# Loads of the start in another order, early products in fours, and half-length conv taps as direct sums

## The chip, the cores and the metric

The kernel runs on one core of one Trainium2 chip. The metric is the device time of one execution in microseconds (us), the median of several. Each engine of the core has its own queue of instructions, run in order: TensorE (PE: matmuls, and transposes as matmuls with an identity), VectorE (DVE), ScalarE (ACT), GpSimd (POOL), and SyncE (SP), which issues the DMAs here. A semaphore holds an instruction, and everything behind it in its queue, until what it needs is done.

## What is computed

Two layers (DEPTH 2) over 1024 tokens of width 1024, in fp32. The lines of the reference that matter (the conv has 31 taps on 512 channels, the one of the feed-forward part 3 taps on 5632):

```python
h = rms_norm(x, pre_mix_norm[l])
z = jnp.einsum("bsd,dc->bsc", h, w_in[l])
...
u = c_a * jax.nn.sigmoid(c_g)
u = causal_dwconv(u, conv_w[l], conv_b[l])
u = jax.nn.silu(layer_norm(u, conv_ln_g[l], conv_ln_b[l]))
...
o = diff_attention(q1, q2, k1, k2, v, lam)
o = rms_norm(o, subln_g[l]) * (1.0 - lam_init)
...
m = jnp.einsum("bsc,cd->bsd", jnp.concatenate([u, o], axis=-1), w_out[l])
x = x + rms_norm(m, post_mix_norm[l])
h = rms_norm(x, pre_ffn_norm[l])
up = jnp.einsum("bsd,df->bsf", h, w_up[l])
up = causal_dwconv(up, ffn_conv_w[l], ffn_conv_b[l])
g, val = jnp.split(up, 2, axis=-1)
f = jnp.einsum("bsf,fd->bsd", jax.nn.gelu(g, approximate=True) * val, w_down[l])
x = x + rms_norm(f, post_ffn_norm[l])
```

## The kernel before

Every fp32 product is three products of rounded parts (high by high, high by low, low by high). A weight is split by ACT, which writes the high part, and by POOL or DVE, which subtracts it for the low part; an activation likewise, with the low part on DVE.

**Start.** Tokens go in 8 tiles of 128 (x0 to x7). `prenorm` takes one: ACT squares it and sums (L357), DVE and POOL make the factor (L347, L349), DVE scales it in place with the gain gb (L359), PE transposes it in 8 pieces (L364), ACT copies the high part (L366) and DVE subtracts for the low part (L367), into hA (tokens 0 to 511) or hB (512 to 1023). The loads of x0 to x2 (into two buffers "y" and one "xr"), of the identity, of gb, of the causal mask nmask, of cos and sin, and of the layer's small parameters (`params`: conv weights, biases, lambda vectors) are issued first on SP, the first weights behind them.

**Mix stage.** It is written through a planner, `Flow`: generators yield the instructions of one piece each, and the planner, with a table of costs per engine, lets a filling queue, timed pieces and the queue of conv taps take turns; the order of PE, DVE, ACT and POOL is what it writes, while SP's order is left to a scheduler. The queue `TAPS = "0a 0b 1w 2w 3a 3b"` gives the conv of the four channel tiles: 0 and 3 as two halves of 512 tokens ("a", "b"), 1 and 2 whole ("w"). A tap piece is let in when DVE's clock in the plan is not ahead of PE's by more than 0.15 to 0.25 us.

`conv_taps` makes the 31-tap sum from even and odd samples (a fast filter for two phases): the sum of even and odd (`xsum`, L573), then three sums A, B and C of 16, 15 and 16 taps on half as many columns (L597), of which ACT makes the first of each (L591), and three instructions that put them together (L600, L603, L606). For a half (512 tokens) these are 48 DVE instructions on about 256 columns and 3 on ACT; for a whole part, on 512 columns. The buffers are two of a ring "y", which x0 and x1 use at the start.

After the taps `conv_fin` transposes, `conv_ln` normalises (z, L1036), and `w_out` (pw, L499) follows with attention beside it. At its end ACT and DVE make yn, the normalised input of the feed-forward stage: its last tiles by L1185.

**Feed-forward stage.** The up-projection takes 22 pairs of columns n, each with seven block products (numbered 1 to 7) in place of eight, on blocks of 512 channels by 512 tokens and their sums. Products 1 and 2 use the first 512 tokens alone (b11 and b21, the two halves of the channels); the others use sums with the second 512 tokens (b22, t1 to t4). For the 8 pairs in `EARLY`, products 1 and 2 are done ahead, as "e1" and "e2", both into the PSUM tile px. They run while yn of the later tokens is made. A product is 12 matmuls of 512 columns in the trace (L1609). `seq` put them two pairs at a time: e1 e1 e2 e2. The transposes of yn's four later tiles (`norm_t`, L1357) stand at the slots `NORM_T` of this sequence; `norm_c` then makes their parts in four steps of DVE and ACT (L1372 to L1391) for the products on t1 to t4 and b22. `e_copy` copies each px to SBUF (ACT L1462, L1464) into one of `ACC_BUFS` = 3 buffers of 1024 columns and, once both halves are there, writes it out with a DMA of 512 KB (L1465), to be fetched again later.

Of the kernel before, what the change touches and what calls it, by code (L numbers as in the profile page):

```python
# [9 lines left out]
F32 = mybir.dt.float32  # L10
F32R = mybir.dt.float32r
AF = mybir.ActivationFunctionType
# [41 lines left out]
NORM_T = (2, 5, 8, 11)  # L54
# [159 lines left out]
def build(tc, ap, out):  # L214
# [7 lines left out]
    with ExitStack() as top:  # L222
# [28 lines left out]
        first_x = lambda t: load_x(xin[t], ("y", "y", "xr")[t % 3])  # L251
# [10 lines left out]
        ve.tensor_copy(nmaskr, nmask)  # L262
        cos = const("cosT", [P, 8, 8])
        sy.dma_start(cos, ap["cos"])
        sin = const("sinT", [P, 8, 8])
        sy.dma_start(sin, ap["sin"])
# [3 lines left out]
        def params(l):  # L270
# [6 lines left out]
            cw, cv, sg = ptile("cw", [P, 4, CK]), ptile("cv", [P, 3, 4]), ptile("sg", [P, 1])  # L277
            sy.dma_start(cw, ap["cw"][l])
            sy.dma_start(cv, ap["cvec"][l])
            sy.dma_start(sg, ap["subg"][l])  # L280
            lv = par.tile([P, 4, HD], F32, tag="lv", name="lv", bufs=1)
            sy.dma_start(lv, ap["lamv"][l:l + 1].broadcast_to([P, 4, HD]))
            cws, hv, ls, nl = ptile("cws", [P, 4, (CK + 1) // 2]), ptile("hv", [P, 2, 4]), ptile("ls", [P, 2]), ptile("nl", [P, 1])
            pars[l] = dict(cw=cw, cws=cws, cv=cv, hv=hv, sg=sg, nl=nl)
# [129 lines left out]
        for l in range(DEPTH):  # L414
            xres = xin if l == 0 else x2[l - 1]
            with ExitStack() as st:
# [4 lines left out]
                if l == 0:  # L421
                    for t in range(8):
                        late[t] = prenorm(ptr, x0[t] if t < 3 else first_x(t), g_pre, hh[t // 4], t % 4)
                if l == 0:
                    for _ in params(0):
                        pass
# [130 lines left out]
                def conv_taps(ct, part):  # L557
# [9 lines left out]
                    n0, n1 = bs[0] * 256, (bs[-1] + 1) * 256  # L567
                    n = n1 - n0
                    c = dv(n, 0.123)
                    iy = yield from R["y"].get()  # L570
                    scr = xs.tile([P, YW], F32, tag="y", name="scr", bufs=2)
                    xsum, bb = scr[:, 0:n + 15], scr[:, n + 15:2 * n + 16]
                    ve.tensor_tensor(xsum, ev[:, n0:n1 + 15], od[:, n0:n1 + 15], op=ALU.add)  # L573
                    fl.op("dve", c)
                    yield 0
                    iac = iy
# [1285 lines left out]
```

## Time and profile before

| | us |
|---|---|
| median of 3 runs (2315.09 to 2317.93) | 2316.41 |
| the profiled execution | 2314.21 |
| its span | 2312.4 |

The profile is of one execution. Its page gives busy time by engine; the windows give busy time in a stretch; the list of waits says what an engine's idle time ended with; the time lines give single instructions, each with its start, its duration and in brackets the idle time ahead of it. An instruction's duration reaches past the start of the next where the engine overlaps them, so the cost of one in a row is the distance between starts.

### The profile page before, as it was taken

What the parts mean: (1) busy time and instruction counts of PE and PEld (TensorE: products, weight loads), DVE (VectorE), ACT (ScalarE), POOL (GpSimd) and SP (SyncE); (2) the same over time, 40 slices, a digit from 0 to 9 for tenths busy, and PEclk for the clock granted to TensorE, in tenths of its full rate; (3) what the DMA queues carried; (4) which work ended last, traced back from release to release, by engine and by line L of the source; (5) the groups of instructions that cost most, each with busy time, mean ns of one, the idle gap of its engine ahead of it and who ended that gap; (6) DMA issues with size and microseconds to landing.
All of it is one profiled execution on the core that took longest, in us unless ns stands there. A gap on an engine that the chain in (4) does not pass through costs nothing. (4 is left out here: it accounts for less than half of the span.)

```text
span 2312.4 us, 31516 instructions
## 1 busy us (share of the span) xinstructions
PE 2202.4 (95%) x10568; PEld 1838.5 (80%) x10568; DVE 1879.3 (81%) x3287; ACT 1126.7 (49%) x2458; POOL 832.6 (36%) x894
## 2 busy tenths in 40 slices
PE   6999997999999999999889999979999999999998
PEld 5898895878877878788778988868788778787886
DVE  6988988667888888777889889896678888887777
ACT  4445456655444444444534545465554444445443
POOL 3324312245444545201533333122454554442024
PEclk9999997999999999999999999979999999999999
DMA  4313323454333343933433123235533343348353
GB/s 156 86 48 92 79 72 123 164 206 138 119 120 130 111 137 130 316 96 111 135 100 103 41 82 97 73 114 191 194 118 124 119 136 123 104 168 274 96 164 118
DMA packets 140129, 295.39 MB, mean 128 GB/s; under 512 B 16832, under 2 KB 33984, under 8 KB 139456
## 3 DMA queue, kind: packets, MB, share of 16 engines
q1 hardware_dynamic: 139968, 293.39, 39.7%
q8 instruction: 83, 1.36, 0.3%
q14 instruction: 78, 0.64, 0.1%
HBM read 198.44 MB, written 78.12 MB: 120 GB/s over the span
## 5 line engine op out<-in xcount | busy, mean ns | idle before, releaser
L1660 PE MATMUL pd<-wp,wo 128*128 128x512 f32 x1776 | 414.2, 395 | 4.8 <-DVE wp L1305 2.8
L1660 PEld LDWEIGHTS pd<-wp,wo 128*128 128x128 f32 x1776 | 333.9, 188 | 81.7 <-DVE wp L1305 3.6
L1609 PE MATMUL py<-t,wo 128*128 128x512 f32 x1584 | 381.8, 394 | 5.8 <-DVE cg L1477 5.8
L1609 PEld LDWEIGHTS py<-t,wo 128*128 128x128 f32 x1584 | 296.8, 188 | 77.4 <-ACT wo L1304 9.0
L1305 POOL TENSOR_TENSOR wo<-ws,wo 128x512 fp32r<-128x512 f32 x176 | 249.9, 1432 | 279.5 <-ACT wo L1304 274.1
L1609 PE MATMUL px<-hA,wo 128*128 128x512 f32 x1056 | 255.3, 394 | 0.0
L1305 POOL TENSOR_TENSOR wo<-raw,wo 128x512 fp32r<-128x512 f32 x132 | 181.4, 1378 | 166.1 <-ACT wo L1304 157.3
L1609 PEld LDWEIGHTS px<-hA,wo 128*128 128x128 f32 x1056 | 198.6, 189 | 44.5 <-ACT ea L1464 0.5
L1305 POOL TENSOR_TENSOR wo<-fa,wo 128x512 fp32r<-128x512 f32 x66 | 103.1, 1577 | 323.0 <-ACT wo L1304 293.9
L1304 ACT ACTIVATE wo<-ws 128x512 fp32r<-128x512 f32 x176 | 108.8, 627 | 136.7 <-PE py L1609 47.4
L1495 DVE SCALAR_TENSOR_TENSOR acc<-cg,fw,acc 128x512 f32<-128x512 f32 x176 | 132.6, 754 | 41.7 <-ACT acc L1483 38.1
L597 DVE SCALAR_TENSOR_TENSOR scr<-u,cw,scr 128x256 f32<-128x256 f32 (+2 forms) x288 | 158.0, 565 | 3.7 <-ACT scr L591 3.6
L852 ACT ACTIVATE e<-S,mxv 128x512 f32<-128x512 f32 (+2 forms) x192 | 110.1, 581 | 64.6 <-DVE mxv L847 41.2
L1483 ACT ACTIVATE acc<-cg,fb,fw 128x512 f32<-128x512 f32 x88 | 68.2, 774 | 148.8 <-DVE cg L1477 148.8
L857 POOL TENSOR_TENSOR sm<-sm 128x1 f32<-128x1 f32 x64 | 25.5, 398 | 316.9 <-ACT e L852 301.6
L499 PE MATMUL pq<-whq,hA 128*128 128x384 f32 x512 | 135.5, 346 | 3.9 <-ACT whq L463 3.9
L499 PE MATMUL pq<-whq,hB 128*128 128x384 f32 x512 | 133.9, 342 | 0.0
L1609 PE MATMUL pz<-b,wo 128*128 128x512 f32 x528 | 129.8, 394 | 1.9 <-DVE cv L1477 1.9
L1609 PE MATMUL pz<-t,wo 128*128 128x512 f32 x528 | 128.7, 392 | 0.0
L1609 PEld LDWEIGHTS pz<-b,wo 128*128 128x128 f32 x528 | 98.4, 188 | 27.4 <-issue 5.1
L843 DVE TENSOR_REDUCE mxv<-S 128x1 f32<-128x512 f32 (+2 forms) x192 | 100.5, 549 | 24.1 <-PE S L827 18.2
L1609 PEld LDWEIGHTS pz<-t,wo 128*128 128x128 f32 x528 | 99.1, 188 | 22.7
(279 smaller groups left out, 5027.2 us busy)
## 6 DMA issues: line engine op xcount, KB each, us to landing
raw<-in_wupd SPq DMA_DIRECT2D x104, 512.0 KB, 3.6
fa<-f SPq DMA_DIRECT2D x154, 256.0 KB, 2.7
f<-fs SPq DMA_DIRECT2D x88, 256.0 KB, 3.3
raw<-in_wmix SPq DMA_DIRECT2D x80, 256.0 KB, 3.0
f<-gg SPq DMA_DIRECT2D x66, 256.0 KB, 2.0
raw<-in_wmix SPq DMA_DIRECT2D x64, 192.0 KB, 2.4
qs<-sth SPq DMA_DIRECT2D x64, 128.0 KB, 2.4
os<-onT SPq DMA_DIRECT2D x16, 512.0 KB, 3.2
```

The source lines that it names most:

```text
L499: mm = pe.matmul(dst, a, b, start=first and k + j == 0, stop=final and k == n - 1 and j == 2)
L597: ve.scalar_tensor_tensor(dst, src, wk, dst, op0=ALU.mult, op1=ALU.add)
L843: ve.tensor_reduce(mv_[:, j:j + 1], S, axis=AX.X, op=ALU.max, negate=True)
L852: se.activation(e[:, c0:c0 + w], S, AF.Exp, bias=mv_[:, 0:1], accum_out=sm[:, j:j + 1])
L857: po.tensor_tensor(sm[:, 0:1], sm[:, 0:1], sm[:, 1:2], op=ALU.add)
L1304: se.activation(w[:, 0], raw, AF.Copy)
L1305: eng.tensor_tensor(w[:, 1], raw, f32(w[:, 0]), op=ALU.subtract)
L1483: se.activation(acc[n, v, hf], C[n][v][:, 2 + hf * HB:2 + hf * HB + HB], AF.Identity, bias=fb[:, mt:mt + 1], scale=fw[:, mt, 2:3])
L1495: ve.scalar_tensor_tensor(dst, c[:, j + hf * HB:j + hf * HB + HB], fw[:, mt, j:j + 1], a, op0=ALU.mult, op1=ALU.add)
L1609: pe.matmul(ps, x, y, start=first and k + j == 0, stop=k == 3 and j == 2, skip_group_check=not first)
L1660: pe.matmul(ps[tt], x, y, start=first and k + n == 0, stop=k == K2 - 1 and n == 2, skip_group_check=not first)
```

## The change

Three parts.

1. Start: x0 to x3 are loaded at once (x3 into the second "xr" buffer). The loads of the parameters, cos, sin and nmask move behind the first four weight loads, and the cast of nmask and the arithmetic on the parameters into a timed piece of the planner.

```diff
-        first_x = lambda t: load_x(xin[t], ("y", "y", "xr")[t % 3])
+        first_x = lambda t: load_x(xin[t], ("y", "y", "xr", "xr")[t % 4])
...
-        x0 += [first_x(1), first_x(2)]
-        nmask = xs.tile([P, P], F32, tag="m0", name="nmask", bufs=4)
-        sy.dma_start(nmask, ap["nmask"])
+        x0 += [first_x(1), first_x(2), first_x(3)]
+        nmask = const("nmask", [P, P])
         nmaskr = const("nmaskr", [P, P], mybir.dt.bfloat16)
-        ve.tensor_copy(nmaskr, nmask)
...
+                def constants():
+                    yield 1.0
+                    next(par0)
+                    sy.dma_start(cos, ap["cos"])
+                    sy.dma_start(sin, ap["sin"])
+                    sy.dma_start(nmask, ap["nmask"])
+                    yield 7.0
+                    next(par0, None)
+                    ve.tensor_copy(nmaskr, nmask)
+                    fl.op("dve", 1.8)
```

2. Taps: the halves ("a", "b") are direct sums over 31 taps on 512 columns, the first on ACT with the bias, 30 on DVE into one accumulator. The whole parts stay.

```diff
+                    if part != "w":
+                        iy = iac = yield from R["y"].get()
+                        acc = xs.tile([P, YW], F32, tag="y", name="acc", bufs=2)[:, 0:HB]
+                        for k in range(CK):
+                            src = us[ct][:, bs[0] * HB + k:(bs[0] + 1) * HB + k]
+                            if k == 0:
+                                se.activation(acc, src, AF.Identity, bias=bias, scale=w(0))
+                                fl.op("act", ac(HB))
+                            else:
+                                ve.scalar_tensor_tensor(acc, src, w(k), acc, op0=ALU.mult, op1=ALU.add)
+                                t = fl.op("dve", dv(HB, 0.123))
+                            yield 0
```

3. Early products: four pairs at a time, each part copied into a buffer of its own (the size of the buffer stays) and written out with a DMA of 256 KB; the transposes' slots move with it.

```diff
-NORM_T = (2, 5, 8, 11)
+NORM_T = (4, 6, 9, 12)
...
-                    seq = [(j, n) for q in range(0, len(early), 2) for j in ("e1", "e2") for n in early[q:q + 2]]
+                    seq = [(j, n) for q in range(0, len(early), 4) for j in ("e1", "e2") for n in early[q:q + 4]]
...
-                        if j == "e1":
-                            eh[n] = up.tile([P, T], F32, tag="acc", name="ea", bufs=ACC_BUFS)
-                            se.activation(eh[n][:, 0:HB], px[n], AF.Copy)
-                        else:
-                            se.activation(eh[n][:, HB:T], px[n], AF.Copy)
-                            sy.dma_start(esp[l][n], eh.pop(n))
+                        e = up.tile([P, T], F32, tag="acc", name="ea", bufs=ACC_BUFS)[:, 0:HB]
+                        se.activation(e, px[n], AF.Copy)
+                        sy.dma_start(esp[l][n][:, 0:HB] if j == "e1" else esp[l][n][:, HB:T], e)
...
-                            px[n] = (pmm.tile([P, HB], F32, tag="mm", name="px") if j == "e1" else
-                                     pO.tile([P, HB], F32, tag="o", name="px"))
+                            q = early.index(n) % 4 if j == "e1" else 2
+                            px[n] = ((pmm if q < 2 else pO if q == 2 else pS)
+                                     .tile([P, HB], F32, tag=("mm", "mm", "o", "S")[q], name="px"))
```

At the start, DVE before, from the factor of x3 to the low parts of x3 (xr_448 and xr_471 are x3 and x4; pt_434 and pt_441 the transposes of x2, pt_457 and pt_464 those of x3):

```order
L347 TENSOR_SCALAR ss_450<-ss_450 128x1
L359 SCALAR_TENSOR_TENSOR xr_448<-xr_448,rs_454,gb0_0_90 128x1024
L367 TENSOR_TENSOR hA_0_372<-pt_434,hA_0_372 128x4x128
L367 TENSOR_TENSOR hA_1_373<-pt_441,hA_1_373 128x4x128
L347 TENSOR_SCALAR ss_473<-ss_473 128x1
L359 SCALAR_TENSOR_TENSOR xr_471<-xr_471,rs_477,gb0_0_90 128x1024
L367 TENSOR_TENSOR hA_0_372<-pt_457,hA_0_372 128x4x128
L367 TENSOR_TENSOR hA_1_373<-pt_464,hA_1_373 128x4x128
```

DVE after, from the factor of x4 on (xr_467 and xr_490 are x4 and x5; pt_432 and pt_439 are of x2, pt_453 and pt_460 of x3):

```order
L344 TENSOR_SCALAR ss_469<-ss_469 128x1
L287 TENSOR_SCALAR hv0_564<-cv0_560 128x8
L356 SCALAR_TENSOR_TENSOR xr_467<-xr_467,rs_473,gb0_0_90 128x1024
L364 TENSOR_TENSOR hA_0_370<-pt_432,hA_0_370 128x4x128
L364 TENSOR_TENSOR hA_1_371<-pt_439,hA_1_371 128x4x128
L344 TENSOR_SCALAR ss_492<-ss_492 128x1
L288 TENSOR_SCALAR sg0_561<-sg0_561 128x1
L289 TENSOR_TENSOR lv_562<-lv_562 128x128
L356 SCALAR_TENSOR_TENSOR xr_490<-xr_490,rs_496,gb0_0_90 128x1024
L364 TENSOR_TENSOR hA_0_370<-pt_453,hA_0_370 128x4x128
L364 TENSOR_TENSOR hA_1_371<-pt_460,hA_1_371 128x4x128
```

The scaling of a tile of x has moved one place up: ahead of the low parts of x2 stands now that of x4, ahead of those of x3 that of x5, with rows of the parameters in between.

In the early products of layer 0, SP before (gb1_0 is the gain of layer 1's first norm, x1_0_7 the last store of the residual, ea buffers of copied products, e_0_1 the place of pair 1's):

```order
L1175 DMA x1_0_7_113<-xe_5570 128x1024 [waits DMAHW2_49,DVE_49]
L247 DMA gb1_0_10737<-in_norms 128x1024 [waits DMAHW3_49,DVE_49]
L1409 DMA raw_5805<-in_wupd 128x1024 [waits DMAHW4_49,Pool_49]
L1465 DMA e_0_1_329<-ea_5787 128x1024 [waits DMAHW5_49,Activation_49]
L1465 DMA e_0_4_332<-ea_5807 128x1024 [waits DMAHW6_49,Activation_49]
```

SP after:

```order
L1185 DMA x1_0_7_111<-xe_5473 128x1024 [waits DMAHW2_49,DVE_49]
L247 DMA gb1_0_10673<-in_norms 128x1024 [waits DMAHW3_49,DVE_49]
L1486 DMA e_0_1_327<-ea_5707 128x512 [waits DMAHW4_49,Activation_49]
L1433 DMA raw_5726<-in_wupd 128x1024 [waits DMAHW5_49,Pool_49]
L1486 DMA e_0_4_330<-ea_5728 128x512 [waits DMAHW6_49,Activation_49]
L1486 DMA e_0_7_333<-ea_5747 128x512 [waits DMAHW7_49,Activation_49]
L1486 DMA e_0_9_335<-ea_5766 128x512 [waits DMAHW0_49,Activation_49]
L1486 DMA e_0_1_327<-ea_5802 128x512 [waits DMAHW1_49,Activation_49]
```

ACT after, at the same place (the fourth copy, of px_5750, is the first that waits for a DMA's semaphore, that of e_0_1):

```order
L1485 ACTIVATE ea_5707<-px_5694 128x512 [waits PE_49,Activation_49]
L1328 ACTIVATE wo_5723<-raw_5665 128x512 [waits Activation_49]
L1485 ACTIVATE ea_5728<-px_5710 128x512 [waits PE_49]
L1328 ACTIVATE wo_5744<-raw_5682 128x512 [waits DMAHW3_49,Activation_49]
L1485 ACTIVATE ea_5747<-px_5731 128x512 [waits PE_49]
L1328 ACTIVATE wo_5763<-raw_5687 128x512 [waits DMAHW4_49,Activation_49]
L1485 ACTIVATE ea_5766<-px_5750 128x512 [waits DMAHW4_49,PE_49,Activation_49]
L1398 ACTIVATE ts_5793<-pt_5769 128x512 [waits PE_49]
L1399 ACTIVATE b22_5654<-pt_5774 128x4x128 [waits PE_49]
```

The writing out of the first product has come to stand directly behind the load of gb1_0, and ACT's copy of the fourth product waits for it; behind that copy stand the first two copies of the transposed yn (pt_5769, pt_5774).

In the taps of the first half, DVE before (scr_704 holds xsum and the sums B, A and C, u_606 the conv's input):

```order
L597 SCALAR_TENSOR_TENSOR scr_704<-u_606,cw0_563,scr_704 128x256 [waits DVE_49]
L597 SCALAR_TENSOR_TENSOR scr_704<-u_606,cw0_563,scr_704 128x257 [waits DVE_49]
L367 TENSOR_TENSOR hB_0_374<-pt_549,hB_0_374 128x4x128 [waits Activation_49]
L367 TENSOR_TENSOR hB_1_375<-pt_556,hB_1_375 128x4x128 [waits Activation_49]
L691 TENSOR_TENSOR v0_750<-pq_696,v0_750 128x128
L597 SCALAR_TENSOR_TENSOR scr_704<-scr_704,cws0_571 128x256 [waits DVE_49]
L597 SCALAR_TENSOR_TENSOR scr_704<-u_606,cw0_563,scr_704 128x256 [waits DVE_49]
```

DVE after (acc_704 is the direct sum):

```order
L572 SCALAR_TENSOR_TENSOR acc_704<-u_588,cw0_559,acc_704 128x512 [waits Activation_49]
L572 SCALAR_TENSOR_TENSOR acc_704<-u_588,cw0_559,acc_704 128x512 [waits DVE_49] x4
L364 TENSOR_TENSOR hB_0_372<-pt_545,hB_0_372 128x4x128 [waits Activation_49]
L364 TENSOR_TENSOR hB_1_373<-pt_552,hB_1_373 128x4x128 [waits Activation_49]
L572 SCALAR_TENSOR_TENSOR acc_704<-u_588,cw0_559,acc_704 128x512 [waits DVE_49]
L701 TENSOR_TENSOR v0_744<-pq_696,v0_744 128x128
L572 SCALAR_TENSOR_TENSOR acc_704<-u_588,cw0_559,acc_704 128x512 [waits DVE_49] x4
L701 TENSOR_TENSOR v0_744<-pq_739,v0_744 128x128 [waits PE_49,Activation_49]
L572 SCALAR_TENSOR_TENSOR acc_704<-u_588,cw0_559,acc_704 128x512 [waits DVE_49] x4
```

Where three sums took turns, one sum now stands with up to six of its taps in a row, each waiting for the one ahead of it.

More of the change, by code (lines that the diff above doesn't have):

```diff
@@ new lines, in conv_taps @@
+                    ev, od = (us[ct].rearrange("p (n two) -> p two n", two=2)[:, i] for i in range(2))
+                    if part == "w":
+                        n0, n1 = bs[0] * 256, (bs[-1] + 1) * 256
+                        n = n1 - n0
+                        c = dv(n, 0.123)
+                        iy = yield from R["y"].get()
+                        scr = xs.tile([P, YW], F32, tag="y", name="scr", bufs=2)
+                        xsum, bb = scr[:, 0:n + 15], scr[:, n + 15:2 * n + 16]
+                        ve.tensor_tensor(xsum, ev[:, n0:n1 + 15], od[:, n0:n1 + 15], op=ALU.add)
+                        fl.op("dve", c)
+                        yield 0
+                        iac = iy
+                        if part == "w":
+                            iac = yield from R["y"].get()
+                            acc = xs.tile([P, YW], F32, tag="y", name="acc", bufs=2)[:, 0:T]
+                        else:
+                            acc = scr[:, 2 * n + 16:YW]
+                        A, C = (acc.rearrange("p (n two) -> p n two", two=2)[:, :, i] for i in range(2))
+                        for m in range((CK + 1) // 2):
+                            for name, dst, src, wk in (("A", A, ev[:, n0 + m:n1 + m], w(2 * m)),
+                                                       ("B", bb, od[:, max(n0 - 1 + m, 0):n1 + m], w(2 * m - 1)),
+                                                       ("C", C, xsum[:, m:n + m], wsum(m))):
+                                first = m == (1 if name == "B" else 0)
+                                if name == "B" and m == 0:
+                                    continue
+                                if first and ACT_TAP:
+                                    se.activation(dst, src, AF.Copy, scale=wk)
+                                    fl.op("act", ac(n))
+                                elif first:
+                                    ve.tensor_scalar(dst, src, wk, None, op0=ALU.mult)
+                                    fl.op("dve", c)
+                                else:
+                                    ve.scalar_tensor_tensor(dst, src, wk, dst, op0=ALU.mult, op1=ALU.add)
+                                    fl.op("dve", c)
+                                yield 0
+                        ve.scalar_tensor_tensor(C, A, bias, C, op0=ALU.subtract, op1=ALU.subtract)
+                        fl.op("dve", c)
+                        yield 0
+                        ve.scalar_tensor_tensor(A, A, bias, bb[:, 0:n], op0=ALU.add, op1=ALU.add)
+                        fl.op("dve", c)
+                        yield 0
+                        ve.scalar_tensor_tensor(C, C, -1.0, bb[:, 1:n + 1], op0=ALU.mult, op1=ALU.subtract)
+                        t = fl.op("dve", c)
+                        yield 0
@@ L1273, in next_params @@
                     next(g)
+                    next(g)
                     yield 220.0
```

58 lines of the change are left out of this document (9 added, 49 removed).

## The prediction

> **What bounds the kernel now.** I read the page first, then the table of windows, then TensorE's list of waits, and last the time lines at the places where the waits lie.
>
> ```profile
> span 2312.4 us, 31516 instructions
> PE 2202.4 (95%) x10568; PEld 1838.5 (80%) x10568; DVE 1879.3 (81%) x3287; ACT 1126.7 (49%) x2458; POOL 832.6 (36%) x894
> PE   6999997999999999999889999979999999999998
> PE 11%; DVE 1%; DMA 0%; issue 0%; POOL 0%; SPq 0%; ACT 0%; DVEq 0%; POOLq 0%
> ```
>
> TensorE is the bound on average: 95% busy, so at most 2312.4 − 2202.4 = 110 us can be had without removing matmuls, and the change removes none. The row of slices (57.8 us each) shows where these 110 us lie: the start, the slice from 347 us, and less clearly near 1100 to 1560 us. The end is far from all edits: the chain that ended last is TensorE's.
>
> ```profile
> 0.00:58.00 58.00, 36.71 (x175) 30.43 (x176) 35.81 (x70) 27.41 (x54) 19.37 (x26) 0.94 0.49 156
> 58.00:174.00 116.00, 114.89 (x673) 105.58 (x672) 101.31 (x233) 50.35 (x151) 30.83 (x44) 1.00 0.25 67
> 350.00:384.00 34.00, 20.40 (x89) 15.57 (x88) 30.67 (x90) 23.95 (x69) 8.14 (x20) 0.70 0.42 123
> 1500.00:1540.00 40.00, 27.23 (x105) 20.11 (x106) 38.35 (x98) 28.17 (x75) 12.43 (x23) 0.63 0.45 137
> 600.00:1100.00 500.00, 494.60 (x2133) 399.43 (x2132) 409.23 (x581) 232.05 (x395) 187.04 (x172) 1.00 0.44 143
> ```
>
> In each row, behind the window and its length, the columns are busy us of PE, PEld, DVE, ACT, POOL, then the granted clock. Most of the mix stage (58:174) and the feed-forward stage (600:1100) are TensorE's; there a DVE instruction more or less costs nothing while DVE has idle time (14.7 of 116 us in the first). Two stretches are DVE's: 350:384 in layer 0 (DVE 90%, PE 60%) and 1500:1540 in layer 1 (96%, 68%). There a microsecond of DVE work is about a microsecond of time.
>
> ```profile
> PE pt L364 <- DVE ss L347: 13.7, 1, 13.7
> PE pt L1357 <- DVE ss L347: 7.8, 2, 3.9
> ...
> PE pq L499 <- ACT whq L463: 3.9, 1, 3.9
> ```
>
> These are the waits that the edits aim at: the start, the early products (3.9 us in each layer), and the start of layer 1.
>
> **Part 1, the start.** It removes nothing; it moves loads.
>
> ```profile
> 11.37 0.23 DVE L262 CAST nmaskr<-nmask 128x128 bf16<-128x128 f32 x1 [6.62 <-DMA nmask<-in_nmask]
> ...
> 12.39 1.28 DVE L359 SCALAR_TENSOR_TENSOR xr<-xr,rs,gb 128x1024 f32<-128x1024 f32 x1 [0.73 <-POOL rs L349]
> ...
> 24.39 1.28 DVE L367 TENSOR_TENSOR hA<-pt,hA 128x512 fp32r<-128x512 f32 x2
> ...
> 26.46 1.28 DVE L359 SCALAR_TENSOR_TENSOR xr<-xr,rs,gb 128x1024 f32<-128x1024 f32 x1 [0.72 <-POOL rs L349]
> 27.66 1.28 DVE L367 TENSOR_TENSOR hA<-pt,hA 128x512 fp32r<-128x512 f32 x2
> 1.65 0.42 SPq L247 DMA_DIRECT2D gb<-in_norms  x1
> gb<-in_norms SPq DMA_DIRECT2D x1, 512.0 KB, 6.9
> 28.40 1.12 PE L364 MATMUL pt<-ident,xr 128*128 128x128 f32 x4 [0.38 <-DVE hA L367]
> ```
>
> Today DVE's first scaling of x (L359) stands behind the cast of nmask, which waits 6.62 us for its load. With the cast moved, that scaling waits for gb alone: 1.65 + 6.9 = 8.55, so 12.39 − 8.55 = 3.8 us earlier. It doesn't reach TensorE whole. By the changed order of DVE (shown with the change) the scaling of x4 now stands ahead of the low parts of x2, and that of x5 ahead of those of x3. Walking that order with these durations (a scaling 1.28 behind about 0.7 us for POOL's power, a pair of low parts 1.28), x0 to x5 are scaled at about 8.6, 12.1, 14.1, 17.5, 21.5 and 24.8, and the low parts of x3 begin at 26.0 instead of 27.66. The transposes of x4 that wait for them (28.40) come 1.7 us earlier, behind them TensorE is dense. **−1.7 us.** Bounds: 0 (the first loads of the weights now share the queue with x) and −6 (if the DVE order did not hold it, more than the 3.8 could be had, since x3 is no longer loaded late). I take the walk, as every duration in it has a row.
>
> **Part 2, the taps of token halves.** A half had 48 DVE instructions on 256 columns and 3 on ACT; now 30 on 512 and one on ACT. There are 8 halves, 4 in each layer; the whole parts are untouched.
>
> ```profile
> 43.76 0.44 DVE L573 TENSOR_TENSOR scr<-u 128x271 f32<-128x271 f32 x1 [0.18 <-PE pt L364]
> ...
> 67.38 0.48 DVE L597 SCALAR_TENSOR_TENSOR scr<-scr,cws 128x256 f32<-128x256 f32 x1
> 67.78 0.48 DVE L597 SCALAR_TENSOR_TENSOR scr<-u,cw,scr 128x256 f32<-128x256 f32 x1
> ...
> 123.57 0.42 DVE L606 SCALAR_TENSOR_TENSOR scr<-scr 128x256 f32<-128x256 f32 x1
> ...
> 504.39 0.74 DVE L1172 SCALAR_TENSOR_TENSOR xe<-m,rs,xe 128x512 f32<-128x512 f32 x1
> 505.05 0.74 DVE L1173 SCALAR_TENSOR_TENSOR xe<-xn,rs,xe 128x512 f32<-128x512 f32 x1
> ...
> 609.80 0.75 DVE L1495 SCALAR_TENSOR_TENSOR acc<-cv,fw,acc 128x512 f32<-128x512 f32 x1
> 610.58 0.75 DVE L1495 SCALAR_TENSOR_TENSOR vv<-cv,fw,acc 128x512 f32<-128x512 f32 x1
> ```
>
> The first row and the one at 123.57 begin and end the taps of the first two halves (43.8 to 124.0, 40 us a half). Narrow taps step 67.78 − 67.38 = 0.40 us from start to start, so a half took 48 × 0.40 = 19.1 us. On 512 columns an independent pair steps 505.05 − 504.39 = 0.66 us. A pair in which the second reads what the first wrote steps 610.58 − 609.80 = 0.78. The three sums of before alternated; the direct sum is one chain. In the changed DVE order, 116 of the 240 half taps stand directly behind a tap, the others have something between. So a half costs 30 × 0.66 + 116/8 × 0.12 = 21.5 us: **2.4 us more of DVE** each, less some 0.4 because fewer taps meet POOL's operations. Beside PE-bound work a half has 14.7 × 40/116 = 5 us of DVE idle time, which hides it; if that cover is gone each half costs up to its 2 us. I take +1.5 us a layer for places where PE waits for DVE at once (bounds 0 and 4).
>
> The Trainium skill, VectorE: DVE Perf Modes, section on the DRAIN, says that the next DVE instruction starts only when the pipe is empty anyway, and that a semaphore between two costs nothing extra. By it the chain term is 0 and a half costs 30 × 0.66 = 19.8; its section of rules for kernel authors asks for fewer instructions, which the change gives. The rows 609.80 and 610.58 against 504.39 and 505.05 speak against it here (0.78 against 0.66), so I keep the 0.12 and hold the rule as a rival.
>
> The planner also places the work anew. Between the last value rows of a layer's qkv and the first normalised conv rows (z), which is where the two DVE-bound stretches lie, I counted in the orders: layer 0, 26 narrow tap instructions and 9 row maxima of 512 columns before, 13 wide taps and 7 maxima after; layer 1, 28 and 11 before, 10 and 7 after. At 0.40 a narrow tap, 0.7 a wide one and 0.68 a maximum that is 16.5 against 13.9 (−2.6), and 18.7 against 11.8 (−6.9). In layer 1 I count two thirds (−4.5), since what moved ahead meets 58 us windows there that already hold 7 us of PE idle time. So the mix stages: layer 0 −2.5 + 1.5 = **−1.0** (−4 to +4), layer 1 −4.5 + 1.5 = **−3.0** (−7 to +4).
>
> At layer 1's start ACT made the split weights that PE waited for (3.9 us) behind two taps, the second of which waited for the sum x_even + x_odd. That sum is gone from halves and one ACT tap of 0.76 us (today's form on 512 columns) stands ahead: **−1.0** (0 to −1.5, beyond which hB is late).
>
> **Part 3, early products.** The number of matmuls stays. Instead of two products ahead of the first transposes of yn there are now four.
>
> ```profile
> 497.71 5.60 PE L1609 MATMUL px<-hA,wo 128*128 128x512 f32 x24
> 507.19 1.94 PE L1357 MATMUL pt<-ident,xn 128*128 128x128 f32 x8 [3.88 <-DVE ss L347]
> 508.79 9.31 PE L1609 MATMUL px<-hA,wo 128*128 128x512 f32 x36
> 517.93 1.03 PE L1357 MATMUL pt<-ident,xn 128*128 128x128 f32 x8
> 518.73 8.55 PE L1609 MATMUL px<-hA,wo 128*128 128x512 f32 x36
> ...
> 553.71 2.50 PE L1609 MATMUL py<-t,wo 128*128 128x512 f32 x10
> ```
>
> Two products last 5.5 us, yn's first tile is ready at 507.05; four last to about 509, so the 3.88 us go. So does the slow clock behind them: 1.94 − 1.03 = 0.9 for the transposes and 9.31 − 8.55 = 0.76 for the products. Up to 5.4 us, if what comes next (the products on t, at 553.71) is ready 5.4 us earlier.
>
> ```profile
> 512.79 0.33 SPq L247 DMA_DIRECT2D gb<-in_norms  x1
> gb<-in_norms SPq DMA_DIRECT2D x2, 512.0 KB, 4.7
> 514.57 1.29 DVE L1372 TENSOR_TENSOR ts<-pt,ts 128x512 f32<-128x512 f32 x2
> 546.27 4.69 DVE L1372 TENSOR_TENSOR t<-ts,t 128x512 fp32r<-128x512 f32 x4
> 1693.23 4.69 DVE L1372 TENSOR_TENSOR t<-ts,t 128x512 fp32r<-128x512 f32 x4
> 1700.66 1.56 PE L1609 MATMUL py<-t,wo 128*128 128x512 f32 x6
> ```
>
> Here the two layers differ. Each copy of a product now has its own DMA from one of three buffers, so the fourth copy waits until the first copy's DMA has landed. In layer 0 that DMA stands in SP's queue behind the load of the next layer's gb, which waits for DVE's last yn and issues at 512.79, landing 4.7 later at 517.5. The fourth copy, ready at about 510.2, waits on ACT until about 518; behind it stand the first step of the norm's transposed tile and the next splits. DVE's step at 514.57 waits for that: +5.4 us. DVE is 97% busy from there to the last of its four norm tiles, so its next to last result (today about 547.4, inside the row of 546.27) comes at 552.8, and the products at 552.6 instead of 553.71: **−1.1** (−5.4 to +1). In layer 1 no gb stands ahead, the first copy's DMA issues at once. DVE's results are ready at 1694.4, the products would arrive at 1700.66 − 5.4 = 1695.3: **−5.2** (−5.4 to −3). From there to the end of the stage PE is dense, so the gain stays.
>
> Sum: −1.7 − 1.0 − 1.1 − 1.0 − 3.0 − 5.2 = **−13.0 us**. The profiled execution took 2314.21 us (span 2312.4 and 1.8 around it), so 2301.2; it lies 2.2 below the median of three, 2316.41. Against the median: **2303 us**.
>
> **Rivals.**
> - *No jam in layer 0, and DVE's order costs less at the start*: 4.3 us more in layer 0 and some 3 more at the start, 2296. For it: other copies' DMAs could land sooner than I think. Against: SP's queue is in order. 0.17.
> - *The chain costs nothing*: a tap behind a tap steps 0.66 us as the independent pair does, a half costs 19.8 − 0.4 = 19.4 us, hardly more than the 19.1 of before, and the +1.5 of each layer goes: 2300. Against it the two pairs of rows. 0.08. (The DRAIN section of the Trainium skill's page VectorE: DVE Perf Modes has it so.)
> - *The jam comes in layer 1 too* (16 DMAs and three buffers, beside the stores of x): 4.1 of its 5.2 us go, 2307. For it: before, a buffer held two copies. 0.12.
> - *The stretches stay as long*, because what DVE doesn't do there it owes just ahead, and the lag stays: 2303 + 8, 2311, no measurable change. 0.12.
> - *Slower*: the direct sums lengthen the DVE-bound halves, 3a and 3b of each layer. If every tap steps 0.78, a half costs 23.4 instead of 19.1 us, +4.3; DVE's idle time there is 3.3 of 34 us and 1.65 of 40, so from about 2 us a half on PE waits for all of it. Four such halves: +17.2 us in place of the mix stage's −4, and 2314.2 − 9.0 + 17.2 = 2322.4, against the median 2324.6. For it: nothing hides DVE there. Against: 124 of 240 taps have something between, and the count of instructions falls. 0.11.
>
> **How the numbers follow.** The forecast has 0.40. About 0.2% (4.6 us) is what a measurement of this kernel can tell from no change. Faster by more, below 2311.8: forecast and the first three rivals, 0.77, less a little for the fourth's edge, 0.76. Within: the fourth, 0.13. Slower: 0.11. The ends of all bounds taken at once would give −29 to +6 us; as they hardly fall together, I take −23 to +2 against the median, 2293 to 2318, which leaves out most of the slower rival and a tail below.
>
> **What would show it.** Start: the first scaling near 8.6 us, the transposes of x4 near 26.7. Taps: a step of 0.66 with something between, 0.78 behind a tap; PE idle time in the two DVE-bound stretches down by 2 to 7 us. Early: no wait of 3.9 at yn's transposes; in layer 0 an idle stretch of ACT of about 8 us ahead of the fourth copy, and PE waiting shortly for t; none in layer 1. It is wrong if PE waits for DVE's taps in 58:174, or if the last conv norm comes late.

## The result, and the profile after

| | before | after |
|---|---|---|
| median, us (4 executions of each) | 2316.04 (2315.09 to 2317.93) | 2345.1 (2342.21 to 2346.77) |
| ratio, 95% interval | | 1.0127 (1.0114 to 1.0139) |
| profiled execution, us | 2314.21 | 2346.77 |
| its span, us | 2312.4 | 2345.0 |

The change makes the kernel 29 us slower. The forecast was 2303 us, with a chance of 0.11 for slower: wrong in sign, and outside the range.

The page of the changed kernel: the span, the busy time of the engines, TensorE's row of slices, and the shares in the chain that ended last.

```profile
span 2345.0 us, 31435 instructions
PE 2215.0 (94%) x10568; PEld 1845.8 (79%) x10568; DVE 1902.7 (81%) x3141; ACT 1121.3 (48%) x2442; POOL 839.5 (36%) x896
PE   6999997898999999999989999979999999999998
PE 11%; DVE 1%; DMA 0%; issue 0%; ACT 0%; POOL 0%; DVEq 0%; POOLq 0%; SPq 0%; ACTq 0%
```

TensorE has the same 10568 matmuls and is busy 12.6 us longer; the other 20 us of the longer span are idle time. DVE has 146 instructions fewer and is busy 23.4 us longer. The list of TensorE's waits says where the idle time lies (in all, times, longest):

```profile
PE pw L496 <- DMA cat<-os: 12.8, 3, 6.1
PE px L1630 <- ACT ea L1485: 12.1, 4, 4.6
...
PE S L834 <- ACT e L862: 8.9, 5, 3.1
...
PE pq L496 <- ACT whq L460: 2.7, 1, 2.7
```

In the profile of before the first of these was 2.5 us, the second wasn't in the list, the third was 5.2, and the fourth 3.9. The waits of yn's transposes (3.9 in each layer) have gone, as they should.

To see which part of the program lost, I cut the span at four places of TensorE's time line: the first early product of each layer (px, 48 matmuls in a row in the changed kernel) and the first product on t (py). Its rows in the changed kernel:

```profile
509.82 11.05 PE L1630 MATMUL px<-hA,wo 128*128 128x512 f32 x48
...
572.94 3.32 PE L1630 MATMUL py<-t,wo 128*128 128x512 f32 x12
...
1675.31 11.05 PE L1630 MATMUL px<-hA,wo 128*128 128x512 f32 x48
...
1731.60 2.97 PE L1630 MATMUL py<-t,wo 128*128 128x512 f32 x12
```

| stretch, us | before | after | difference | forecast |
|---|---|---|---|---|
| start and mix of layer 0, to px | 497.71 | 509.82 | +12.1 | −2.7 |
| early products of layer 0, px to py | 56.00 | 63.12 | +7.1 | −1.1 |
| feed-forward of layer 0 and mix of layer 1, py to px | 1091.10 | 1102.37 | +11.3 | −4.0 |
| early products of layer 1, px to py | 55.85 | 56.29 | +0.4 | −5.2 |
| the rest | 611.7 | 613.4 | +1.7 | 0 |

These are single profiles. Five profiles whose mix code is that of before (before itself, E3, E5, E12, E13) reach px at 496.8 to 502.5 and take 1088.6 to 1091.6 for the third stretch, so 6 us in the first line and 3 in the third are what one profile can differ by.

### The profile page after: what moved, and what is told of

Read it like the earlier page. It is cut to its first block, busy times and chain, and to the rows that moved or that the text cites. A ratio compares the mean times of both kernels' runs of the same rounds, so it can differ in the third digit from the quotient of the medians.

```text
span 2345.0 us, 31435 instructions
## 1 busy us (share of the span) xinstructions
PE 2215.0 (94%) x10568; PEld 1845.8 (79%) x10568; DVE 1902.7 (81%) x3141; ACT 1121.3 (48%) x2442; POOL 839.5 (36%) x896
## 5 line engine op out<-in xcount | busy, mean ns | idle before, releaser
L1630 PE MATMUL px<-hA,wo 128*128 128x512 f32 x1056 | 260.5, 399 | 12.1 <-ACT ea L1485 12.1
L1630 PEld LDWEIGHTS px<-hA,wo 128*128 128x128 f32 x1056 | 201.1, 191 | 58.9 <-ACT ea L1485 13.8
L572 DVE SCALAR_TENSOR_TENSOR acc<-u,cw,acc 128x512 f32<-128x512 f32 x240 | 197.8, 824 | 11.5 <-ACT acc L569 7.5
L1328 ACT ACTIVATE wo<-raw 128x512 fp32r<-128x512 f32 x132 | 81.7, 625 | 62.6 <-PE pw L496 15.5
```

The lines of the kernel that those rows point to most:

```text
L572: ve.scalar_tensor_tensor(acc, src, w(k), acc, op0=ALU.mult, op1=ALU.add)
L1328: se.activation(w[:, 0], raw, AF.Copy)
L1630: pe.matmul(ps, x, y, start=first and k + j == 0, stop=k == 3 and j == 2, skip_group_check=not first)
```

## Experiments

Every version ran beside the kernel of before on its chip; the ratio is to that kernel, its 95% interval in brackets. About 0.2% can be told from no change.

### The three parts alone

E1 is the kernel of before with part 1 (the start) alone, E2 with part 2 (the taps) alone, E3 with part 3 (the early products) alone, E4 with parts 1 and 3; the edits are those of the diff.

> The kernel before with the start's part alone (loads moved, x0 to x3 at once). Theory A (the direct sums, by the planner's new order, and the early products by their copies, are what costs; the start is harmless): PE's order outside the start is that of before, so 1 to 3 us faster than before, about 2314. Rival B (the start's timed pieces and moved parameters upset the mix stage): 10 us or more slower than before.

> The kernel before with the direct sums of the halves alone. Theory A: the last head's transposes of layer 0 stand behind 213 instead of 174 matmuls of w_out, PE waits some 6 us twice for that head's output, and layer 1's mix stage grows as in the changed kernel by about 10: 18 to 26 us slower than before, about 2338. Rival B: within 5 us of before.

> The kernel before with the early products in fours alone. From the changed kernel's trace, theory A: the copies jam ACT, in layer 0 behind the load of gb (8 us) and in both layers at the second group of four, so 5 to 9 us slower than before, about 2323; layer 0 loses most. Rival C (the jam is only there because the mix stage came out late): 5 us faster than before, about 2311.

> The changed kernel with the taps of halves as before (start and early products changed). Theory A: the sum of the two alone, 4 to 8 us slower than before, some 23 us faster than the changed kernel. If the parts do not add, it differs from that sum by over 3 us.

| | median, us | ratio |
|---|---|---|
| before, on this chip | 2313.49 | |
| E1 start | 2316.76 | 1.0008 (0.9998 to 1.0019) |
| E2 taps | 2336.17 | 1.0097 (1.0082 to 1.0112) |
| E3 early products | 2321.01 | 1.0028 (1.0015 to 1.0041) |
| E4 start and early | 2325.36 | 1.0049 (1.0032 to 1.0065) |

0.08 + 0.97 + 0.28 = 1.33%, against 1.27% for the whole change: the parts add up within their intervals. The taps cost some 22 us, the early products 6, the start nothing that can be measured. No part gains. E2 and E3 came as expected. E1 missed the gain of 1 to 3 us that theory A gave it, and E4 lost 11.9 us, more than the 4 to 8 expected, but about what E1 and E3 lose together (10.8 by the medians).

### Taps: which halves, and is it DVE's work?

E6 has direct sums in the halves of channel tile 0 only, E7 in those of tile 3 only, the halves that lie in the two DVE-bound stretches. The others keep the fast filter.

```diff
-                    if part != "w":
+                    if part != "w" and ct == 0:
...
-                    if part == "w":
+                    if part == "w" or ct != 0:
```

This is E6; E7 has 3 in place of 0.

> Direct sums for the halves of channel tile 0 alone, tile 3's halves by the fast filter as before. Theory P (the loss of the direct sums is the planner's new order at the mix stage's end: the last head's transposes, behind 213 matmuls of w_out in layer 0 where they stood behind 174): here they stand behind 90 in both layers, so within 4 us of before. Rival W (each direct half costs its extra DVE work and chain): half of e2's loss, 9 to 13 us slower.

> Direct sums for the halves of channel tile 3 alone. Theory P: the last head's transposes stand behind 159 (layer 0) and 156 (layer 1) matmuls of w_out, 174 and 141 before: within 5 us of before. Rival W: half of e2's loss or more, 9 to 20 us slower, since these halves lie in the stretches that DVE bounds.

E8 is the kernel of before, fast filter and all: the arithmetic is unchanged, but the planner takes the taps of a half two at a time, about the length of a direct tap. (In the order that came of it, six weight splits stand on POOL that were DVE's.) It asks whether the coarser piece alone moves the time.

```diff
-                            yield 0
+                            taps += 1
+                            if part == "w" or taps % 2 == 0:
+                                yield 0
```

> The kernel before, in which the planner lets the taps of halves in two at a time (0.80 us of DVE at once, as one direct tap takes 0.78), the arithmetic and the DVE work unchanged. If the larger piece of DVE work ahead of the attention's small steps is the loss (rival G), 8 to 20 us slower than before; theory P with the last head's transposes behind 159 and 156 matmuls, and rival W with unchanged work: within 4 us.

| | median, us | ratio |
|---|---|---|
| before, on this chip | 2315.02 | |
| E6 tile 0 | 2317.72 | 1.0009 (1.0000 to 1.0018) |
| E7 tile 3 | 2329.73 | 1.0060 (1.0044 to 1.0076) |
| E8 fast filter, pieces of two | 2327.29 | 1.0050 (1.0034 to 1.0066) |

The loss sits in tile 3. E7 (+14.7 us) went against theory P, which had it within 5 us, and came as its rival had it, which blamed DVE's extra work. E8 speaks for the order: it loses 12 us by the planner's new order, with DVE busy 1880.4 us in place of 1879.3. Its waits are of the same kinds as those of E2. First E2, then E8:

```profile
PE pw L499 <- DMA cat<-os: 14.1, 3, 6.0
...
PE S L837 <- ACT e L865: 9.2, 4, 3.1
```

```profile
PE pw L499 <- DMA cat<-os: 9.8, 2, 5.6
PE S L827 <- ACT e L855: 7.6, 5, 2.8
```

### Taps: the chain, the planner's number, the planner's lead

Each is E2 with one thing changed. E9 splits the sum into two, which alternate and are added at the end, so that no tap reads what the one ahead of it wrote. E10 leaves the arithmetic and tells the planner a longer tap (0.25 in place of 0.123 in its cost formula). E11 leaves both, and lets a tap in near the end of the mix, when fewer than 12 pieces are left in the filling queue, only if DVE's planned clock is at most 0.15 us ahead of PE's, not 0.25.

```diff
+                        accs = acc[:, 0:HB], acc[:, HB:2 * HB]
+                            s = accs[k % 2]
-                                ve.scalar_tensor_tensor(acc, src, w(k), acc, op0=ALU.mult, op1=ALU.add)
+                                ve.scalar_tensor_tensor(s, src, w(k), s, op0=ALU.mult, op1=ALU.add)
...
+                        ve.tensor_tensor(acc, acc, accs[1], op=ALU.add)
```

```diff
-                                t = fl.op("dve", dv(HB, 0.123))
+                                t = fl.op("dve", dv(HB, 0.25))
```

```diff
-    AHEAD2 = 0.25
+    AHEAD2 = 0.15
```

> Direct sums of all halves as in e2, but odd and even taps go into two accumulators (ACT makes the first of each, DVE adds them at the end), so that neighbouring taps do not depend on each other; the number of DVE instructions of a half stays 30. Theory N (the chain's 0.12 us per tap, and the plan's ignorance of it, is a main part of e2's loss): 2324 to 2330, 8 or more of e2's 22 us go. Rival G (the plan's order and the size of the pieces are the loss): e2's loss stays within 5 us.

> Direct sums as in e2; only the planner's cost of such a tap is raised from 0.66 to the measured 0.78 us, so the code's work is the same and its order differs (last head's transposes behind 117 matmuls of w_out in layer 0, 141 in layer 1). If the plan's error on the chain is the loss: 8 us or more of e2's 22 go. If the DVE work itself is: within 4 us of e2.

> Direct sums as in e2; the planner lets a tap in when DVE is at most 0.15 us ahead of PE instead of 0.25, so the last head's transposes stand behind 111 matmuls of w_out in layer 0 instead of 213, and 153 instead of 141 in layer 1. Theory P (order of the last head): layer 0's wait for that head's output of 6 us goes and with it 8 to 12 us, layer 1 stays: about 2326. If DVE work is the loss: as e2, about 2336.

E15 is the kernel of before with E11's lead of 0.15, and E16 is E9 with it.

> The kernel before with the planner's lead of e11 (0.15 instead of 0.25 us), nothing else. If the lead is better whatever the taps, 5 us or more faster than before. If e11's lead mends only what the larger taps did to the order: within 5 us of before, or slower.

> e11's lead with e9's two accumulators. If order and chain are the two causes and they add: 4 us faster than e11, so about as fast as before (2313 to 2315). If the chain is hidden once the order is mended: as e11.

| | median, us | before, on this chip | ratio |
|---|---|---|---|
| E9 two sums | 2332.19 | 2314.33 | 1.0079 (1.0064 to 1.0094) |
| E10 longer tap in the plan | 2324.32 | 2314.33 | 1.0046 (1.0029 to 1.0063) |
| E11 lead 0.15 | 2317.38 | 2314.33 | 1.0013 (1.0003 to 1.0022) |
| E15 before, lead 0.15 | 2323.94 | 2315.69 | 1.0039 (1.0025 to 1.0053) |
| E16 two sums, lead 0.15 | 2320.41 | 2315.69 | 1.0021 (1.0010 to 1.0032) |

E10 does the work of E2 and, as expected if the plan's error is the loss, gets back 0.51 of its 0.97%, some 12 of 22 us; E11 does the same 3141 DVE instructions and gets back 0.84, some 19 us, more than expected, since layer 1's stretch came down too. Its list of TensorE's waits has no row for the DMA of cat, and the attention's is 6.3 us:

```profile
PE S L837 <- ACT e L865: 6.3, 7, 2.5
```

E15 says that 0.15 is no better number: the kernel of before loses 8 us with it, and not by waits for cat, of which its list has none. I read this as a match of lead and piece; that the order of before is simply a good one, and that most other orders lose, isn't excluded. E9 stands 0.18% below E2, about 4 us, which the two intervals (0.82 to 1.12 and 0.64 to 0.94) don't separate; with the order mended (E16 against E11, 3 us slower) nothing of it is seen. So no gain from breaking the chain is shown; E11, which keeps the chain, is within 3 us of before by the medians.

The same cuts as above, from the time lines of these kernels:

| us | to px, layer 0 | py to px, layer 1 |
|---|---|---|
| before | 497.7 | 1091.1 |
| E2 taps | 509.6 | 1099.2 |
| E7 tile 3 | 506.5 | 1099.0 |
| E8 pieces of two | 504.1 | 1097.3 |
| E10 longer tap in the plan | 502.2 | 1093.5 |
| E11 lead 0.15 | 497.5 | 1090.9 |

### Early products: the jam, the load of gb, the group of four

E5 is E3 with the copies two to a buffer again (e1 and e2 go into the halves of one, each still with a DMA of its own), so that three buffers hold six copies.

```diff
-                        e = up.tile([P, T], F32, tag="acc", name="ea", bufs=ACC_BUFS)[:, 0:HB]
+                        if not eh:
+                            eh[0] = up.tile([P, T], F32, tag="acc", name="ea", bufs=ACC_BUFS)
+                            e = eh[0][:, 0:HB]
+                        else:
+                            e = eh.pop(0)[:, HB:T]
```

> The early products in fours alone, but two copies share one of the three buffers (its two halves), so six copies fit and only the seventh waits for a landed DMA. Theory A (three buffers and the wait for a DMA's landing are the loss of e3): no long wait of ACT at the fourth copy, 5 to 9 us faster than before, about 2307. Rival D (the copies come late because they stand behind the norm's steps in ACT's queue, whatever the buffers): still 3 to 7 us slower than before.

E12 is E5 with the load of layer 1's gb held back in SP's queue, by a write to its tile on POOL ahead of it.

```diff
+            if l == 1 and i == 0:
+                po.memset(t[:, 0:1], 0.0)
```

> As e5 (early products in fours alone, two copies to a buffer), and the load of layer 1's first gain waits for a small write in layer 0's down stage, so that it no longer stands in SP's queue ahead of the weight loads and copies. If that load is what is left of the loss: layer 0's early stage 4 to 5 us shorter than in e5, 2 to 5 us faster than before. If the second group of four is: within 1.5 us of e5.

E13 is E12 with the first four pairs as a group and the other four in twos, as before. E14 is E13 with the start of the change.

```diff
-                    seq = [(j, n) for q in range(0, len(early), 4) for j in ("e1", "e2") for n in early[q:q + 4]]
+                    seq = [(j, n) for g in (early[0:4], early[4:6], early[6:8]) for j in ("e1", "e2") for n in g]
```

> As e12, but only the first group is four pairs, the other four pairs go two at a time as before. If the waits for PSUM banks of the second group were the loss: no wait of PE for a copied px, 4 to 10 us faster than before. If DVE's chain of norm steps sets the end whatever the order: within 2 us of e12.

> e13 with the start's part of the change. If the start is neutral (e1: 0.08% slower, not told from none): as e13 within 2 us. If its early gain of 2 us lasts where nothing else disturbs: 2 us faster than e13.

| | median, us | before, on this chip | ratio | px to py, layer 0 and 1 |
|---|---|---|---|---|
| before | | | | 56.0, 55.9 |
| E3 early products | 2321.01 | 2313.49 | 1.0028 (1.0015 to 1.0041) | 61.1, 57.1 |
| E5 two copies a buffer | 2316.79 | 2315.02 | 1.0009 (0.9996 to 1.0022) | 60.1, 56.8 |
| E12 and gb late | 2314.81 | 2314.96 | 0.9998 (0.9990 to 1.0007) | 56.8, 56.8 |
| E13 four, then twos | 2317.01 | 2314.96 | 1.0003 (0.9994 to 1.0013) | 57.1, 58.3 |
| E14 and the start | 2318.52 | 2314.96 | 1.0014 (1.0005 to 1.0022) | |

E5 freed ACT of the wait for a buffer, but in layer 0 another took its place: a weight split that waits for its load, which stands behind that of gb. ACT's time line in E5:

```profile
520.70 0.63 ACT L1304 ACTIVATE wo<-raw 128x512 fp32r<-128x512 f32 x1 [6.80 <-DMA raw<-in_wupd]
```

With gb out of the way (E12) nothing of the loss is left, but nothing is gained either, though TensorE reaches yn's first transposes without a wait. Two expectations missed here: E5 was to be 5 to 9 us faster than before, E12 2 to 5. E13 is 2 us from E12, as expected if DVE's chain sets the end, and E14's start adds no gain. No version here is faster than the kernel of before.

## Why the prediction was wrong

**The start, −1.7: 0.** DVE's time line in the changed kernel, first the scalings of x (L356) and what stands between:

```profile
8.87 1.28 DVE L356 SCALAR_TENSOR_TENSOR xr<-xr,rs,gb 128x1024 f32<-128x1024 f32 x1 [2.96 <-DMA gb<-in_norms]
...
17.33 1.28 DVE L356 SCALAR_TENSOR_TENSOR xr<-xr,rs,gb 128x1024 f32<-128x1024 f32 x1 [0.72 <-POOL rs L346]
...
19.73 1.33 DVE L283 TENSOR_SCALAR cw<-cw 128x124 f32<-128x124 f32 x1
...
22.17 1.28 DVE L356 SCALAR_TENSOR_TENSOR xr<-xr,rs,gb 128x1024 f32<-128x1024 f32 x1 [0.64 <-POOL rs L346]
...
25.44 2.28 DVE L356 SCALAR_TENSOR_TENSOR xr<-xr,rs,gb 128x1024 f32<-128x1024 f32 x1 [0.47 <-POOL rs L346]
27.64 1.27 DVE L364 TENSOR_TENSOR hA<-pt,hA 128x512 fp32r<-128x512 f32 x2
```

The walk holds to x3 (17.33, forecast 17.5). Then the parameters' scaling takes 1.33 us and x5's scaling 2.28, where the profile of before has 0.21 and 1.28 for them. So the low parts of x3 begin at 27.64, not 26.0; before, 27.66. POOL's time line shows what lies beside them:

```profile
18.35 2.63 POOL L466 TENSOR_TENSOR wlw<-raw,whw 128x512 fp32r<-128x512 f32 x2 [1.06 <-ACT whw L460]
...
25.37 1.27 POOL L466 TENSOR_TENSOR wlw<-raw,whw 128x512 fp32r<-128x512 f32 x1
```

The weights now come earlier than the parameters, so POOL splits them at the very time at which DVE scales, and both DVE instructions lie beside such a split. The walk took durations from a trace in which they had been alone. That the split stretches them is read from the times, not tried by itself; in E4 and E14 the parameters' scaling has its 0.21 again, and the copy behind it, now beside the split, takes 1.12 in place of 0.16. That the start gains nothing rests on E1's timed runs (between 0.5 us faster and 4.4 slower), which leave 1.7 us out: a single profile can't show so little, since TensorE's first wait is 12.0 us in E8 and E11 and 13.8 in E5, all three with the start of before.

**The taps' arithmetic, about +2.0 of DVE a half: right in the difference.** The group of the direct taps, and a run of them that lies alone and one beside POOL's splits (DVE's time line):

```profile
L572 DVE SCALAR_TENSOR_TENSOR acc<-u,cw,acc 128x512 f32<-128x512 f32 x240 | 197.8, 824 | 11.5 <-ACT acc L569 7.5
```

```profile
43.17 6.37 DVE L572 SCALAR_TENSOR_TENSOR acc<-u,cw,acc 128x512 f32<-128x512 f32 x5
...
53.58 3.10 DVE L572 SCALAR_TENSOR_TENSOR acc<-u,cw,acc 128x512 f32<-128x512 f32 x4
```

Taking 0.74 for the last, a tap behind a tap steps (3.10 − 0.74)/3 = 0.79, as forecast (0.78). By the Trainium skill (VectorE: DVE Perf Modes, the section on the DRAIN) a semaphore between two DVE instructions costs nothing extra. Read so, the step would be that of an independent pair, 0.66; this trace speaks against that once more. DVE's busy time on E2's page is 1894.2, 14.9 more than before: 1.9 for each of eight halves in the mean. That this meets the forecast so well is partly luck. The direct taps are busy 24.7 us a half (197.8/8), not the 21.5 that the steps gave, as some lie beside POOL's splits; those of before must have been above 19.1 too. The 0.4 us taken off for POOL had no row behind it.

**The mix stages, −1.0 and −3.0: +12 and +11. This is the step that failed.** The prediction said "The planner also places the work anew", and went on to count in the orders how many taps and maxima of DVE stand in the DVE-bound stretches. It looked at one engine, and at amounts. The windows of the first DVE-bound stretch and of two others in layer 0, in the changed kernel:

```profile
350.00:384.00 34.00, 25.33 (x102) 18.84 (x102) 31.21 (x70) 24.94 (x65) 10.75 (x20) 0.65 0.51 162
396.00:402.00 6.00, 2.72 (x6) 2.15 (x7) 1.52 (x5) 0.00 (x0) 0.00 (x0) 0.52 0.27 87
456.00:470.00 14.00, 6.03 (x29) 4.40 (x28) 6.95 (x14) 5.31 (x10) 2.04 (x4) 0.80 0.82 298
```

In 350:384 TensorE does more than before (25.33 against 20.40 us), as was forecast; in layer 1, where the same work stands some 23 us later, 1523:1563 has 29.48 us of TensorE against 27.23 in 1500:1540 before. In layer 0 it loses behind that stretch, at 396 and 456, where in the kernel of before there was little to wait for (1.9 us and nothing). TensorE's time line there, and then SP's queue:

```profile
399.28 1.22 PE L496 MATMUL pw<-whq,cat 128*128 128x512 f32 x2 [5.29 <-DMA cat<-os]
...
456.23 0.60 PE L985 MATMUL pto<-ident,osb 128*128 128x128 f32 x4
467.21 1.22 PE L496 MATMUL pw<-whq,cat 128*128 128x512 f32 x2 [6.09 <-DMA cat<-os]
```

```profile
458.36 0.33 SPq L220 DMA_DIRECT2D os<-onT  x1
...
462.17 0.53 SPq L220 DMA_DIRECT2D cat<-os  x1
```

The last head's output is transposed (pto, 456.23), written to memory (os) and fetched again (cat), and w_out (pw) can use it at 467.21: 11 us from one to the other, in which TensorE needs other w_out work. In the order of before 174 matmuls of w_out stand ahead of these transposes, in the new one 213. In the kernel of before, TensorE's time line shows what stood behind them instead:

```profile
446.02 0.60 PE L975 MATMUL pto<-ident,osb 128*128 128x128 f32 x4
...
448.55 0.62 PE L499 MATMUL pw<-whw,cat 128*128 128x512 f32 x2
449.00 0.39 PE L499 MATMUL pw<-wlw,cat 128*128 128x512 f32 x1
449.23 0.62 PE L499 MATMUL pw<-whq,cat 128*128 128x512 f32 x2
```

Three of them step 0.68 us, so the 39 that moved ahead are 39/3 x 0.68 = 8.8 us of work, which had covered the trip; now 6.1 us of it are idle. The last head isn't the only place. Of w_out, 9 matmuls stood ahead of the transposes of the head before it (388.34 before, 385.22 after), now 18, and the wait for that head at 399.28 is 5.29 us in place of 1.88. In E7 and E8, where only 159 stand ahead of the last head's, this is the place that loses: 33 stand ahead of the head before it, in both layers, and TensorE waits 3.76 and 5.56 us there in layer 0, 6.57 and 4.28 in layer 1. E8's two waits:

```profile
406.29 1.22 PE L499 MATMUL pw<-whq,cat 128*128 128x512 f32 x2 [5.56 <-DMA cat<-os]
...
1556.16 1.22 PE L499 MATMUL pw<-whq,cat 128*128 128x512 f32 x2 [4.28 <-DMA cat<-os]
```

In E10 and E11 none stand ahead of that head's, and 117 and 111 ahead of the last head's: no wait for cat is left. Why the planner moved them I read from its rule: a tap is let in while DVE's planned clock is at most the lead ahead of PE's, and a piece of twice the length overshoots that by more, so that all that shares DVE with the taps, attention first, takes its turn at another point.

In layer 1 of the changed kernel the last head's transposes stand where they stood (141), and the wait for cat is 1.4 us; there the coarser steps show in another place. TensorE waits 8.3 us in three waits of its scores for ACT's exponentials (1.3 us before, between 1380 and 1645). The last of them on TensorE's time line, and DVE's ahead of it:

```profile
1565.93 0.45 PE L834 MATMUL S<-kk2B,qs 128*128 128x384 f32 x1 [3.12 <-ACT e L862]
```

```profile
1560.11 3.10 DVE L572 SCALAR_TENSOR_TENSOR acc<-u,cw,acc 128x512 f32<-128x512 f32 x4
1563.12 1.15 DVE L853 TENSOR_REDUCE mxv<-S 128x1 f32<-128x512 f32 x2
...
1564.26 0.73 DVE L572 SCALAR_TENSOR_TENSOR acc<-u,cw,acc 128x512 f32<-128x512 f32 x1
1564.91 0.15 DVE L857 TENSOR_TENSOR mxv<-mxv 128x1 f32<-128x1 f32 x1
```

The row maxima that the exponentials need stand behind four taps, 3.0 us, and the step that joins them behind a fifth. That DVE's order is the cause in layer 1 is read from this trace; that the planner's order and not DVE's work makes most of the loss is what E8 (12 us with the work of before) and E11 (19 us back with the work of E2) show. What each wait of layer 1 is worth was not tried by itself.

**Layer 1's start, −1.0: −1.2** in the list of waits (3.9 to 2.7).

**Early products of layer 0, −1.1: +7.1.** The jam is as forecast: ACT's fourth copy waited 8.43 us, forecast 8.

```profile
530.60 0.60 ACT L1485 ACTIVATE ea<-px 128x512 f32<-128x512 f32 x1 [8.43 <-DMA e<-ea]
```

What it costs was mis-sized, since the step from there to the end left out two things. First, e1 and e2 share the PSUM tile px, so TensorE itself waits for the copy. TensorE and then ACT, in the changed kernel:

```profile
559.92 4.60 PE L1630 MATMUL px<-hA,wo 128*128 128x512 f32 x12 [4.58 <-ACT ea L1485]
567.65 5.49 PE L1630 MATMUL px<-hA,wo 128*128 128x512 f32 x12 [3.13 <-ACT ea L1485]
```

```profile
558.75 0.63 ACT L1328 ACTIVATE wo<-ws 128x512 fp32r<-128x512 f32 x1 [4.04 <-DVE ws L1444]
559.29 0.58 ACT L1485 ACTIVATE ea<-px 128x512 f32<-128x512 f32 x1
```

In the second group of four the copy stands on ACT behind a weight split that waits 4.04 us for a sum on DVE (ws), and DVE is in the middle of the norm's steps. E12, without the load of gb and with six copies in three buffers, brought px to py of layer 0 down from E3's 61.1 to 56.8.

**Early products of layer 1, −5.2: +0.4.** Second, and worth more: DVE sets the end. The gain assumed that, with TensorE 5.4 us ahead, the products on t come as much earlier. But ACT's copies of px stand among the norm's steps, which go by DVE's chain, and this begins when yn's tile is ready, not when TensorE has its head start. E12, without jam and gb, shows it free of both, here in layer 0. The first step of that chain on DVE:

```profile
512.67 0.68 DVE L1374 TENSOR_TENSOR ts<-pt,hA 128x512 f32<-128x512 f32 x1
```

Before, the same step began at 512.69. TensorE's head start turns into a wait ahead of the last early product, for a copy that stands on ACT behind a step of the norm that waits for DVE (TensorE, then ACT):

```profile
549.25 5.49 PE L1612 MATMUL px<-hA,wo 128*128 128x512 f32 x12 [3.89 <-ACT ea L1467]
554.53 3.09 PE L1612 MATMUL py<-t,wo 128*128 128x512 f32 x12
```

```profile
546.52 1.67 ACT L1387 ACTIVATE t<-ts 128x512 fp32r<-128x512 f32 x3 [1.59 <-DVE ts L1374]
548.10 0.61 ACT L1306 ACTIVATE wo<-ws 128x512 fp32r<-128x512 f32 x1
548.62 0.57 ACT L1467 ACTIVATE ea<-px 128x512 f32<-128x512 f32 x1
```

py at 554.53, before 553.71; DVE's last result on t is done at 553.1, before at 551.0. Layer 1 of E12 has the same wait (3.89, at 1695.82), that of the changed kernel 4.18 (1727.15). The prediction had the bound in its hands (DVE's results "ready at 1694.4" in layer 1, which is the end of the first of the four in that row; the last ends at 1697.9), but took the matmuls between as work that can always run, and didn't follow their px back through ACT to DVE. E13 shows the wait only moving when the second half goes in twos.

**The rivals.** *Slower* had the sign and the place: tile 3's halves, in the DVE-bound stretches (E7). Its mechanism, DVE's own work at 0.78 a tap, had the step right but is at most a part: E11 has the same work and loses 3 us. *The jam in layer 1 too* hardly came: ACT's copy waits 2.15 us for a DMA there, 8.43 in layer 0. The gain there (px to py is 55.85 before and 56.29 after) went by the wait for the copy above. *The stretches stay as long* didn't come: 350:384 holds more of TensorE's work than before, and the loss lies behind it. (Giving back the 2.5 and the 4.5 us would have made it 2310, not 2311.) *No jam* and *the chain costs nothing* are out by the rows above (8.43 us on ACT; 0.79 a tap).

## What to carry to other kernels

When a planner sets the order, a change of a piece's length is a change of the order on every engine: compare the new order against the old at each trip through memory and each hand-over between engines, and ask how much independent work is left behind it, not only how much stands where the bound engine is. A wait on the busiest engine is worth its length only if what comes next doesn't itself end at another engine's chain: follow that chain to where it begins before counting the gain. Durations from a trace hold for the neighbours that they had there; a load moved earlier brings its own work beside theirs.

## What the hardware showed that was not expected

DVE instructions beside a split on POOL took much longer: a tap 6.37/5 = 1.27 us a piece at 43 us, where POOL is in a group of splits from 43.61 on, against 3.10/4 = 0.78; the scaling of x 2.28 against 1.28; the parameters' scaling 1.33 against 0.21. That the split is the cause is read from the times.

After an idle time of 5 to 6 us two w_out matmuls took 1.22 us in place of 0.62, with a granted clock of 0.52 in 396:402. Here the wait cost more than its length. How much of the 12.6 us of longer busy time comes from such waits is open: E2, with 14.1 us of waits for cat, is busy 2204.9 us, 2.5 more than before, and E13, with 2.9 of them, 2211.9.

A load lands at different times in different profiles. In E1 the first scaling of x begins at 7.16 us, in the changed kernel at 8.87, both as soon as gb has landed; all that follows is as much earlier, and x5's scaling, with the same 2.28 us, stands at 23.71 instead of 25.44. Read alone, E1's trace seemed to gain 1.8 us at the start; its timed runs show none.
